# Two token halves side by side: one 512-column pass for two in q, r, the gates and the branch output projections

## The chip, the cores and the metric

One core of one Trainium2 chip runs the whole kernel. The metric is device microseconds of one launch, the median of several runs. TensorE multiplies, ScalarE (ACT) and VectorE (DVE) work element by element, GpSimd (POOL) and SyncE (SP) mostly issue transfers. Matrix products end in PSUM, whose banks hold 512 fp32 columns each.

## What is computed

One hybrid block over 256 latent tokens and 256 context tokens with 2048 channels: a modulated norm, one input projection into two mixers (GLA with 4 heads, SSD with 8 groups), a projection of each mixer's output, sigmoid gates that merge the two, an output projection, and then a product-key expert layer. Cut to what the change touches:

```
h = modulate(rmsnorm(x, w), shift, scale)
q, k, v, r, ..., z, xbc, ..., gl = split(h @ w_in)
o   = rmsnorm(o_gla) * gla_norm_w * silu(r)
y_a = o @ w_gla_out                 # 2048 -> 2048
y_b = y @ w_ssd_out                 # 4096 -> 2048
ga, gb = split(sigmoid(gl + b_gate))
out = (ga * y_a + gb * y_b) @ w_o
```

All of it is fp32. The kernel multiplies in a rounded fp32 format and keeps the precision by splitting each operand into a high part (the rounded value) and a low part (the rest). A product is then three matmuls: high x high, high x low, low x high.

## The kernel before

**Weights.** All large weights come through one `Stream` (line 27) in a fixed plan, in chunks of 128 x 1024 fp32 (512 KB): a chunk is 8 weight tiles of 128 x 128. `get` hands out a chunk and, before that, issues the load of the chunk six ahead (SyncE's queue) and the split of the chunk three ahead: ScalarE writes `hi` (line 49), VectorE writes `lo` = raw - hi (line 50). There are four `hi` and four `lo` buffers, so the split of a chunk waits until TensorE is done with the chunk four before it.

**Products.** `mm3` (lines 320 to 326) goes through the 8 tiles of a chunk and issues three matmuls for each: weight high x token high (324), weight high x token low (325), weight low x token high (326), all into the same columns of PSUM. The normalized tokens are `Hhi` and `Hlo`, 16 tiles of 512 columns each: latent tokens in columns 0 to 255 (`XT`), context tokens behind them. k, xs and B use all 512 columns (`CT`); q, r, z, C and the gates use 256. v (`v_part`, lines 332 to 334) has the tokens as stationary operand and weights of 512 columns moving.

**Banks.** Four PSUM banks rotate under the tag mm. `pair` (line 949) computes two feature tiles of 256 columns into the two halves of one bank; a unit "r" takes two pairs, a unit "v" takes four banks at once.

**Order.** `units` is a list of work written out by hand: for heads 1 to 3 it is k, k, q of the head, r of the head before, v of the head; then r of the last head; then eight groups of SSD units (xs, one gl, xs, C, xs, B, xs, z, z); then the last eight gl. After each chunk `tick` calls `step`, which first moves every background generator on by one step (GLA, decay of the next head, SSD, conv, transfers back) and after that runs the functions in `later`. `q_out`, `r_out` and `gl_out`, which empty the banks of a finished unit, go through `later`; so they are issued in the tick after the first chunk of the next unit. After that `tick` issues a ride: one product on VectorE of a modulation weight that rides along (line 368). Every engine works through its instructions in the order of issue.

**After the units.** `split_in` brings the GLA and SSD outputs back from DRAM and splits them into `yh` and `yl` (lines 986 and 987). `oproj` multiplies them, 2 chunks a feature tile for GLA and 4 for SSD, and `gated` multiplies the bank with the sigmoid of the gates (line 1070) on VectorE. Then come w_o, and the expert layer with 512-column matmuls at its end (lines 1489 to 1491).

**Lines that the prediction names.** 560: a small GLA product that waits for products on VectorE (550). 962: Silu of r out of PSUM. 969: gate plus bias out of PSUM. 494 to 503: decay on VectorE. 583: a sum in GLA. 1254: a reduction in the expert layer. 760: an operation on PSUM in SSD. 1127: sums of squares before the second norm.

Of the kernel before, what the change touches and what calls it, by code (L numbers as in the profile page):

```python
# [10 lines left out]
F32 = mybir.dt.float32  # L11
F32R = mybir.dt.float32r
U32 = mybir.dt.uint32
AF = mybir.ActivationFunctionType
OP = mybir.AluOpType
AX = mybir.AxisListType
# [3 lines left out]
P = 128  # L20
D = 2048
T = 256
KT = D // P
# [71 lines left out]
def hybrid_block_kernel(ctx, tc, A, out):  # L95
    nc = tc.nc
    ctx.enter_context(tc.manual_schedule())
    mm_ = nc.tensor.matmul
# [5 lines left out]
    st = Stream(nc, streams, 6, 3)  # L104

    def mmbank(shape=(P, 512)):
        return psum.tile(list(shape), F32, name="mm", tag="mm", bufs=4)
# [4 lines left out]
    def cload(name, shape):  # L112
        t = consts.tile(list(shape), F32, name=name)
        nc.gpsimd.dma_start(t, A[name])
        return t
# [86 lines left out]

    es_h = ExitStack()
    hpool = es_h.enter_context(tc.tile_pool(name="hh", bufs=1))
    Hhi = hpool.tile([P, KT, 512], F32R, name="Hhi")
    Hlo = hpool.tile([P, KT, 512], F32R, name="Hlo")
    es_w = ExitStack()
    w4 = es_w.enter_context(tc.tile_pool(name="w4", bufs=1, reuse_waits="tile"))
    es_x = ExitStack()
# [36 lines left out]
    b_gate = cload("b_gate", [P, 32])  # L246
# [72 lines left out]
    def mm3(ps, W2, h0, n, hi, lo, tok, start, stop):  # L319

        Whi, Wlo = (w.rearrange("p (k f) -> p k f", f=P) for w in W2)
        for j in range(n):
            k = h0 + j
            mm_(ps, Whi[:, j, :], hi[:, k, tok], start=start and j == 0, stop=False)  # L324
            mm_(ps, Whi[:, j, :], lo[:, k, tok], start=False, stop=False)  # L325
            mm_(ps, Wlo[:, j, :], hi[:, k, tok], start=False, stop=stop and j == n - 1)  # L326

    def v_part(pv, W2, k, j):
        Whi, Wlo = W2
        for tb in range(4):  # L330
            tok = slice(P * tb, P * tb + P)
            mm_(pv[tb], Hhi[:, k, tok], Whi[:, j, :], start=k == 0, stop=False)  # L332
            mm_(pv[tb], Hhi[:, k, tok], Wlo[:, j, :], start=False, stop=False)  # L333
            mm_(pv[tb], Hlo[:, k, tok], Whi[:, j, :], start=False, stop=k == KT - 1)  # L334

    def v_weights():
        return [w.rearrange("p (k f) -> p k f", k=2) for w in st.get()]
# [14 lines left out]
    def tick(riding=True):  # L352
        nonlocal ticks
        step()
        ticks += 1
        st.board()
        if riding and st.aboard and ride_n < 240:
            ride_piece()
# [30 lines left out]
    XT, CT = slice(0, 256), slice(0, 512)  # L389
# [5 lines left out]
    for k, a, b in START:  # L395
# [16 lines left out]
        elif k == "ld":  # L412
# [5 lines left out]
            for w, pp in enumerate((plr, pdt)):  # L418
                Whi, Wlo = (t[:, w, kt % 4] for t in ld)
# [26 lines left out]
    o_d = dram.tile([P, KT, T], F32, name="o_d")  # L446
    y_d = dram.tile([P, 32, T], F32, name="y_d")
# [6 lines left out]
    S = 1.0 / 16.0  # L454
# [4 lines left out]
    Qt, Vt, Rt, Bt, Xt, Ct, Zt, Bm = {}, {}, {}, {}, {}, {}, {}, {}  # L459
# [468 lines left out]
    def pair():  # L928
        ps = mmbank((P, 2, 256))
        for e in range(2):  # L930
            ftile(ps[:, e], XT)
        return ps

    def wait(what):
        while what not in ended:
            step()
# [16 lines left out]

    def q_out(a, ps):
        Qt[a] = wt("s2", [P, 2, 256])
        nc.scalar.activation(Qt[a], ps, AF.Copy, scale=S)

    def r_out(a, pr):
        Rt[a] = []
        for ps in pr:  # L960
            t = wt("s2", [P, 2, 256])
            nc.scalar.activation(t, ps, AF.Silu)
            Rt[a].append(t)
        nc.scalar.preload_act_table_set(NLE)

    def gl_out(a, ps):
        t = op.tile([P, 2, 256], F32, name="mt", tag="mt", bufs=2) if op else wt("s2", [P, 2, 256])
        for e in range(2):
            nc.scalar.activation(t[:, e], ps[:, e], AF.Identity, bias=b_gate[:, 2 * a + e:2 * a + e + 1])
        nc.gpsimd.dma_start(g_d[:, 2 * a:2 * a + 2], t)  # L970


    es_o = ExitStack()
    op = None
    ohi, olo, yhi, ylo, G = [], [], [], [], []

    def split_in(pool, src, n, hi, lo):
        for i in range(n // 4):
            t = op.tile([P, 4, T], F32, name="yr", tag="yr", bufs=2)
            nc.gpsimd.dma_start(t, src[:, 4 * i:4 * i + 4])  # L980
            if i % 2 == 0:
                hi.append(pool.tile([P, 8, T], F32R, name="yh", tag="yh", bufs=n // 8))
                lo.append(pool.tile([P, 8, T], F32R, name="yl", tag="yl", bufs=n // 8))
            s = slice(4 * (i % 2), 4 * (i % 2) + 4)
            yield
            nc.scalar.activation(hi[-1][:, s], t, AF.Copy)
            nc.vector.tensor_sub(lo[-1][:, s], t, hi[-1][:, s].bitcast(F32))

    def open_out():
        nonlocal op  # L990
# [10 lines left out]
    def to_out():  # L1001
        while ("y", 7) not in ended:
            yield
        open_out()
        yield from split_in(op, o_d, 16, ohi, olo)

    for u in units:
        kind, a, b = u
        if kind == "k":
            if b == 0 and a > 1:  # L1010
                Kt[a] = wt("s4", [P, 2, 512])
            ps = mmbank()
            ftile(ps, CT, int(a < 2))
            later.append(lambda a=a, b=b, ps=ps: k_out(a, b, ps))
        elif kind == "q":
            ps = pair()
            later.append(lambda a=a, ps=ps: q_out(a, ps))
        elif kind == "v":
            pv = [mmbank() for _ in range(4)]
            for i in range(8):  # L1020
                w2 = v_weights()
                for j in range(2):
                    v_part(pv, w2, 2 * i + j, j)
                tick()
            wait(("gla", a - 1))
            v_evac(a, pv)
        elif kind == "r":
            pr = [pair(), pair()]
            later.append(lambda a=a, pr=pr: r_out(a, pr))
        elif kind in ("xs", "B", "C"):  # L1030
            nx = 1 if kind == "C" else 2
            ps = mmbank()
            ftile(ps[:, :256 * nx], CT if nx == 2 else XT)
            f = 4 * a + b if kind == "xs" else 32 + a if kind == "B" else 40 + a
            o = wt("s1" if nx == 1 else "s2", [P, 256 * nx])
            bg.append(conv(ps, f, nx, o))
            if kind == "xs":
                Xt.setdefault(a, []).append(o)
            elif kind == "B":
                Bm[a] = o  # L1040
            else:
                Ct[a] = o
        elif kind == "z":
            Zt.setdefault(a, []).append(pair())
            if b == 1:
                if a:
                    wait(("ssd", a - 1))
                later.append(lambda a=a: silu_group(a))
                if a == 7:
                    bg.append(to_out())  # L1050
        elif kind == "gl":
            ps = pair()
            later.append(lambda a=a, ps=ps: gl_out(a, ps))
    drain()
    es_h.close()
# [7 lines left out]
    yp = es_y.enter_context(tc.tile_pool(name="yp", bufs=1, reuse_waits="tile"))  # L1063

    def gated(n, t, ps):

        gate_load(n + 2)
        if n < 15:
            nc.scalar.activation(G[1], G[1], AF.Sigmoid)
        nc.vector.tensor_mul(t, ps, G.pop(0))  # L1070

    def oproj(ps, hi, lo):
        n = len(hi)
        for h in range(n):
            mm3(ps, st.get(), 0, 8, hi[h], lo[h], slice(0, 256), h == 0, h == n - 1)

    ysplit = split_in(yp, y_d, 32, yhi, ylo)
    nc.scalar.activation(G[0], G[0], AF.Sigmoid)
    for i in range(8):
        ps = mmbank((P, 2, 256))  # L1080
        for e in range(2):
            oproj(ps[:, e], ohi, olo)
            next(ysplit, None)
        t = mp.tile([P, 2, T], F32, name="ma", tag="mx", bufs=8)
        gated(i, t, ps)
        Ma.append(t)
        step()
    for i in range(8):
        ps = mmbank((P, 2, 256))
        for e in range(2):  # L1090
            oproj(ps[:, e], yhi, ylo)
        t = op.tile([P, 2, 256], F32, name="mt", tag="mt", bufs=2)
        s = slice(2 * i, 2 * i + 2)
        gated(8 + i, t, ps)
        nc.vector.tensor_add(t, t, Ma.pop(0))
        h = mp.tile([P, 2, T], F32R, name="Mhi", tag="mx", bufs=8)
        nc.scalar.activation(h, t, AF.Copy)
        nc.vector.tensor_sub(Mlo[:, s], t, h.bitcast(F32))
        Mhi.append(h)
# [29 lines left out]
    for i in range(8):  # L1129
        ps = mmbank((P, 2, 256))  # L1130
# [6 lines left out]
        for e in range(2):  # L1137
            k = 2 * i + e
            nc.vector.scalar_tensor_tensor(x1[:, k], ps[:, e], mods[:, 0, 32 + k:33 + k], x1[:, k], op0=OP.mult, op1=OP.add)
        s = slice(2 * i, 2 * i + 2)  # L1140
# [19 lines left out]
    for k in range(KT + 2):  # L1160
# [4 lines left out]
        if k > 1:  # L1165
            j = k - 2
# [172 lines left out]
    for j, e, h in QORD:  # L1339
        if j < 2:  # L1340
            pq.setdefault((j, e), mmbank((P, 256)) if h == 0 else None)
        elif e == 0 and h == 0:
            t = mmbank((P, 2, 256))
# [119 lines left out]
    for b in range(NB):  # L1463
# [4 lines left out]
        for group in ([0], [1], [2], [3]) if b < NB - 1 else ([0], [1], [2, 3]):  # L1468
# [6 lines left out]
            ps, W2 = {}, {}  # L1475
            for order in ([(t, i, j) for i in group for j in range(2) for t in range(2)] if len(group) == 1 else
                          [(t, i, j) for t in range(2) for i in group for j in range(2)]):
                t, i, j = order
# [7 lines left out]
                for k in range(2):  # L1486
                    Whi, Wlo = (w[:, k] for w in W2[i, j])
# [87 lines left out]
```

## Time and profile before

| | us |
|---|---|
| median of 3 runs | 3643.9 |
| lowest, highest | 3643.74, 3644.59 |
| profiled execution | 3642.91 |
| its span, first to last instruction | 3641.1 |
| TensorE busy in it | 3546.8 |
| VectorE busy | 2369.1 |
| ScalarE busy | 1667.7 |

Times in rows are microseconds from the start of the span, durations in ns where marked so. An engine's busy time counts any instant with an instruction in flight; matmuls overlap, so a row of 0.28 us can be followed by the next start 0.12 us later. A bracket behind a row is the idle time of the engine before it and what ended it.

### The profile page before, as it was taken

How to read it: one execution, taken by the hardware profiler on the slowest of the kernel's cores; microseconds unless marked ns; L12 is line 12 of the kernel's file. 1: busy time of each engine (PE TensorE's matmuls, PEld its weight loads, DVE VectorE, ACT ScalarE, POOL GpSimd, SP SyncE). 2: the span in 40 equal slices, each digit the busy share in tenths (PEclk: the TensorE clock that was granted, in tenths of full speed). 3: DMA queues.
4: the chain of work that ended last, by engine and by line, in shares of the span. 5: the costliest groups of instructions: out<-in, count | busy, mean ns of one | idle time of the engine just before them, and what ended most of it. 6: DMA issues, size and time to landing. Idle time of an engine off the chain costs nothing.

```text
span 3641.1 us, 58912 instructions
## 1 busy us (share of the span) xinstructions
PE 3546.8 (97%) x23679; PEld 3182.4 (87%) x23679; DVE 2369.1 (65%) x3569; ACT 1667.7 (46%) x2226; POOL 369.9 (10%) x424
## 2 busy tenths in 40 slices
PE   5989999999999999999999999999999999999998
PEld 2578999888888888999998999999999999998886
DVE  3375665677777776656544788875555555556777
ACT  2244454355555555555433446464444444444444
POOL 0000000000000000010002016361000000000004
PEclk9999999999999999999999999999999999999999
DMA  7744555656655554467667557677666666666774
GB/s 270 263 142 158 179 166 180 194 165 206 207 195 180 180 190 150 156 222 254 194 207 234 162 178 202 196 205 223 197 197 197 198 198 198 198 197 205 235 234 146
DMA packets 214145, 715.39 MB, mean 196 GB/s; under 512 B 24688, under 2 KB 24832, under 8 KB 213360
## 3 DMA queue, kind: packets, MB, share of 16 engines
q1 hardware_dynamic: 188928, 625.04, 53.3%
q0 software_dynamic: 24944, 86.59, 8.7%
q8 instruction: 186, 3.05, 0.3%
q14 instruction: 87, 0.71, 0.1%
HBM read 679.93 MB, written 31.60 MB: 195 GB/s over the span
## 4 chain that ended last, share of the span: by engine, by line
PE 90%; DVE 5%; DMA 3%; ACT 1%; issue 1%; SPq 0%; POOL 0%; DVEq 0%; ACTq 0%; POOLq 0%
PE mm L324 19%; PE mm L326 19%; PE mm L325 19%; PE mm L1490 6%; PE mm L1489 6%; PE mm L1491 6%; PE mm L332 2%; PE sc L1296 2%; PE mm L334 2%; PE mm L333 2%; DVE lo L50 1%; PE sc L866 1%; PE sc L607 1%; PE sc L799 1%; DMA x_d<-x 1%
## 5 line engine op out<-in xcount | busy, mean ns | idle before, releaser
L50 DVE TENSOR_TENSOR lo<-raw,hi 128x1024 fp32r<-128x1024 f32 x996 | 1234.9, 1246 | 1044.4 <-ACT hi L49 1040.7
L49 ACT ACTIVATE hi<-raw 128x1024 fp32r<-128x1024 f32 x996 | 1046.8, 1058 | 1410.8 <-PE mm L325 640.1
L324 PE MATMUL mm<-Hhi,hi 128*128 128x256 f32 (+1 forms) x2272 | 735.3, 324 | 2.2 <-ACT hi L49 1.4
L326 PE MATMUL mm<-Hhi,lo 128*128 128x256 f32 (+1 forms) x2272 | 722.0, 318 | 0.9 <-DVE lo L50 0.9
L325 PE MATMUL mm<-Hlo,hi 128*128 128x256 f32 (+1 forms) x2272 | 721.9, 318 | 0.0
L324 PE MATMUL mm<-h2hi,hi 128*128 128x256 f32 x2304 | 656.3, 285 | 0.0
L325 PE MATMUL mm<-h2lo,hi 128*128 128x256 f32 x2304 | 651.9, 283 | 1.6 <-DVE h2lo L1167 1.1
L326 PE MATMUL mm<-h2hi,lo 128*128 128x256 f32 x2304 | 651.1, 283 | 0.0
L324 PEld LDWEIGHTS mm<-Hhi,hi 128*128 128x128 f32 x2272 | 433.3, 191 | 38.2 <-issue 5.5
L325 PEld LDWEIGHTS mm<-Hlo,hi 128*128 128x128 f32 x2272 | 433.4, 191 | 30.4 <-issue 1.9
L326 PEld LDWEIGHTS mm<-Hhi,lo 128*128 128x128 f32 x2272 | 433.0, 191 | 30.6 <-DVE lo L50 1.2
L325 PEld LDWEIGHTS mm<-h2lo,hi 128*128 128x128 f32 x2304 | 441.2, 191 | 5.8 <-DVE h2lo L1167 2.6
L324 PEld LDWEIGHTS mm<-h2hi,hi 128*128 128x128 f32 x2304 | 440.9, 191 | 4.1 <-ACT h2hi L1164 0.8
L326 PEld LDWEIGHTS mm<-h2hi,lo 128*128 128x128 f32 x2304 | 440.9, 191 | 0.0
L1490 PE MATMUL mm<-lo,ph 128*128 128x512 f32 x1024 | 405.9, 396 | 4.5 <-DVE lo L50 4.5
L1489 PE MATMUL mm<-hi,ph 128*128 128x512 f32 x1024 | 406.1, 397 | 0.0
L1491 PE MATMUL mm<-hi,pl 128*128 128x512 f32 x1024 | 404.8, 395 | 0.0
L1490 PEld LDWEIGHTS mm<-lo,ph 128*128 128x128 f32 x1024 | 192.7, 188 | 48.6 <-DVE lo L50 6.0
L1491 PEld LDWEIGHTS mm<-hi,pl 128*128 128x128 f32 x1024 | 192.8, 188 | 46.5
L1489 PEld LDWEIGHTS mm<-hi,ph 128*128 128x128 f32 x1024 | 193.0, 188 | 43.0
L326 PE MATMUL mm<-yh,lo 128*128 128x256 f32 x768 | 217.0, 283 | 1.5 <-DVE lo L50 1.5
L324 PE MATMUL mm<-yh,hi 128*128 128x256 f32 x768 | 216.9, 282 | 0.7 <-ACT hi L49 0.7
(337 smaller groups left out, 4558.4 us busy)
## 6 DMA issues: line engine op xcount, KB each, us to landing
raw<-in_w_f_dram SPq DMA_DIRECT2D x288, 512.0 KB, 3.7
raw<-in_u_dram SPq DMA_DIRECT2D x256, 512.0 KB, 4.1
raw<-in_v_dram SPq DMA_DIRECT2D x256, 512.0 KB, 4.1
ride<-in_w_ada_dram SPq DMA_DIRECT2D x240, 256.0 KB, 4.0
raw<-in_w_so_dram SPq DMA_DIRECT2D x64, 512.0 KB, 4.1
raw<-in_w_ada_dram SPq DMA_DIRECT2D x45, 512.0 KB, 6.8
raw<-in_w_v_dram SPq DMA_DIRECT2D x32, 512.0 KB, 3.6
s<-cum_d POOLq DMA_DIRECT2D x64, 256.0 KB, 6.3
```

Source lines behind the costliest of these rows:

```text
L49: self.nc.scalar.activation(hi, t, AF.Copy)
L50: self.nc.vector.tensor_sub(lo, t, hi.bitcast(F32))
L324: mm_(ps, Whi[:, j, :], hi[:, k, tok], start=start and j == 0, stop=False)
L325: mm_(ps, Whi[:, j, :], lo[:, k, tok], start=False, stop=False)
L326: mm_(ps, Wlo[:, j, :], hi[:, k, tok], start=False, stop=stop and j == n - 1)
L332: mm_(pv[tb], Hhi[:, k, tok], Whi[:, j, :], start=k == 0, stop=False)
L333: mm_(pv[tb], Hhi[:, k, tok], Wlo[:, j, :], start=False, stop=False)
L334: mm_(pv[tb], Hlo[:, k, tok], Whi[:, j, :], start=False, stop=k == KT - 1)
L1296: mm_(pg[:, j], o1[:, j], o2[:, j], start=True, stop=True)
L1489: mm_(ps[t, i], ghi, Whi, start=j == 0 and k == 0, stop=False)
L1490: mm_(ps[t, i], ghi, Wlo, start=False, stop=False)
L1491: mm_(ps[t, i], glo, Whi, start=False, stop=j == 1 and k == 1)
```

## The change

For q, r, the gates and both branch output projections the high and the low token part lie side by side in one tile, and one matmul of 512 columns takes the high weight part over both: columns 0 to 255 of the bank collect products with the high part, columns 256 to 511 those with the low part. The low weight part still takes 256 columns, into the lower half. The order of the last two is turned so that the 512-column matmul is last. A feature tile so fills a whole bank, and a pair two banks. The halves are added on VectorE by a reduction (`both`) out of PSUM into SBUF, before ScalarE's copy, Silu or bias, or before the product with the gate. `Hhi` and `Hlo` become views of one tile `H`, in which high and low of a row tile lie 512 columns apart. `z`, `C`, the 512-column units, v, w_o and the expert layer stay.

```diff
-    Hhi = hpool.tile([P, KT, 512], F32R, name="Hhi")
-    Hlo = hpool.tile([P, KT, 512], F32R, name="Hlo")
+    H = hpool.tile([P, KT, 2, 512], F32R, name="H")
+    Hhi, Hlo = H[:, :, 0], H[:, :, 1]
...
+    def mm2(ps, W2, h0, x, start, stop):
+        Whi, Wlo = (w.rearrange("p (k f) -> p k f", f=P) for w in W2)
+        for j in range(8):
+            k = h0 + j
+            last = stop and j == 7
+            for w in (Wlo, Whi) if last else (Whi, Wlo):
+                if w is Whi:
+                    mm_(ps, w[:, j, :], x[:, k], start=start and j == 0, stop=last)
+                else:
+                    mm_(ps[:, 0:256], w[:, j, :], x[:, k, 0], start=False, stop=False)
+
+    def both(out, ps):
+        nc.vector.tensor_reduce(out, ps.rearrange("p (s t) -> p t s", s=2), axis=AX.X, op=OP.add)
...
+    def wide_pair():
+        pss = []
+        for e in range(2):
+            pss.append(mmbank())
+            for h in range(2):
+                mm2(pss[e], st.get(), 8 * h, H[:, :, :, XT], h == 0, h == 1)
+                tick()
+        return pss
...
     def q_out(a, ps):
         Qt[a] = wt("s2", [P, 2, 256])
-        nc.scalar.activation(Qt[a], ps, AF.Copy, scale=S)
+        for e in range(2):
+            both(Qt[a][:, e], ps[e])
+        nc.scalar.activation(Qt[a], Qt[a], AF.Copy, scale=S)
...
-        for ps in pr:
+        for h in range(2):
             t = wt("s2", [P, 2, 256])
-            nc.scalar.activation(t, ps, AF.Silu)
+            for e in range(2):
+                both(t[:, e], pr[h][e])
+            nc.scalar.activation(t, t, AF.Silu)
...
         for e in range(2):
-            nc.scalar.activation(t[:, e], ps[:, e], AF.Identity, bias=b_gate[:, 2 * a + e:2 * a + e + 1])
+            both(t[:, e], ps[e])
+            nc.scalar.activation(t[:, e], t[:, e], AF.Identity, bias=b_gate[:, 2 * a + e:2 * a + e + 1])
...
-                hi.append(pool.tile([P, 8, T], F32R, name="yh", tag="yh", bufs=n // 8))
-                lo.append(pool.tile([P, 8, T], F32R, name="yl", tag="yl", bufs=n // 8))
+                to.append(pool.tile([P, 8, 2, T], F32R, name="y2", tag="y2", bufs=n // 8))
...
         elif kind == "q":
-            ps = pair()
+            ps = wide_pair()
...
-            pr = [pair(), pair()]
+            pr = [wide_pair(), wide_pair()]
...
         elif kind == "gl":
-            ps = pair()
+            ps = wide_pair()
...
-        nc.vector.tensor_mul(t, ps, G.pop(0))
+        for e in range(2):
+            both(t[:, e], ps[e])
+        nc.vector.tensor_mul(t, t, G.pop(0))
...
+    def oproj(x):
+        ps = mmbank()
+        for h in range(len(x)):
+            mm2(ps, st.get(), 0, x[h], h == 0, h == len(x) - 1)
+        return ps
```

## Rows read from the trace of the kernel before

**Rows 1.** The page: busy time by engine, and the chain that ended last.
```profile
PE 3546.8 (97%) x23679; PEld 3182.4 (87%) x23679; DVE 2369.1 (65%) x3569; ACT 1667.7 (46%) x2226; POOL 369.9 (10%) x424
...
PE 90%; DVE 5%; DMA 3%; ACT 1%; issue 1%; SPq 0%; POOL 0%; DVEq 0%; ACTq 0%; POOLq 0%
```

**Rows 2.** Busy time in stretches (PE, PEld, DVE, ACT, POOL); timeline of TensorE.
```profile
1720.00:1800.00 80.00, 80.00 (x669) 80.00 (x669) 40.27 (x37) 31.94 (x35) 1.61 (x3) 1.00 0.64 194
3400.00:3480.00 80.00, 80.00 (x344) 64.43 (x343) 57.54 (x64) 32.83 (x32) 6.27 (x12) 1.00 0.75 247
...
348.84 0.39 PE L324 MATMUL mm<-Hhi,hi 128*128 128x512 f32 x1
...
351.79 0.39 PE L325 MATMUL mm<-Hlo,hi 128*128 128x512 f32 x1
```

**Rows 3.** Timeline of TensorE from k (512 columns) to q (256).
```profile
370.37 0.39 PE L326 MATMUL mm<-Hhi,lo 128*128 128x512 f32 x1
370.60 0.28 PE L324 MATMUL mm<-Hhi,hi 128*128 128x256 f32 x1
```

**Rows 4.** Instructions by line and shape: count, busy us, mean ns, idle before.
```profile
L324 PE MATMUL mm<-Hhi,hi 128*128 128x256 f32 x1536 | 443.3, 289 | 1.4 <-ACT hi L49 1.4
```

**Rows 5.** Timeline of TensorE and VectorE in q and r of the first heads.
```profile
260.92 0.75 DVE L368 SCALAR_TENSOR_TENSOR ride<-ride,cS 128x512 f32<-128x512 f32 x1 [2.52 <-DMA ride<-in_w_ada_dram]
...
265.37 1.13 PE L560 MATMUL sc<-s,s 128*128 128x128 f32 x8 [2.12 <-DVE s L550]
...
274.43 1.40 PE L560 MATMUL sc<-s,s 128*128 128x128 f32 x7 [2.19 <-DVE s L550]
```

**Rows 6.** Groups by line: a reduction, and an operation on PSUM.
```profile
L1254 DVE TENSOR_REDUCE tok<-eq 128x64 f32<-128x1024 f32 x8 | 9.7, 1207 | 0.0
L760 DVE TENSOR_TENSOR s<-sc,tm 128x512 f32<-128x512 f32 x64 | 41.1, 683 | 13.1 <-PE sc L754 13.1
```

**Rows 7.** Timeline from r of head 0 to v of head 1.
```profile
293.85 0.40 PE L332 MATMUL mm<-hi,Hhi 128*128 128x512 f32 x1
...
296.96 0.50 PE L332 MATMUL mm<-hi,Hhi 128*128 128x512 f32 x1 [1.55 <-ACT s L962]
...
295.03 1.23 DVE L50 TENSOR_TENSOR lo<-raw,hi 128x1024 fp32r<-128x1024 f32 x1 [0.16 <-ACT hi L49]
```

**Rows 8.** Timeline from r of head 1 to v of head 2.
```profile
421.62 0.58 PE L332 MATMUL mm<-hi,Hhi 128*128 128x512 f32 x1
...
426.40 0.67 DVE L502 TENSOR_TENSOR_SCAN s<-ones,s 128x255 f32<-128x255 f32 x1
```

**Rows 9.** Timeline from r of head 2 to v of head 3.
```profile
539.19 0.58 PE L332 MATMUL mm<-hi,Hhi 128*128 128x512 f32 x1
...
543.15 0.66 DVE L502 TENSOR_TENSOR_SCAN s<-ones,s 128x255 f32<-128x255 f32 x1
```

**Rows 10.** Timeline from r of head 3 to the first xs.
```profile
609.62 0.40 PE L324 MATMUL mm<-Hhi,hi 128*128 128x512 f32 x1
...
612.75 0.42 DVE L583 TENSOR_TENSOR s<-Df,Db 128x256 f32<-128x256 f32 x1
```

**Rows 11.** Stretches (the figure after POOL is the granted clock); waits of TensorE.
```profile
265.00:272.00 7.00, 6.63 (x56) 6.67 (x56) 4.97 (x12) 5.94 (x15) 0.00 (x0) 1.00 0.54 185
275.00:278.00 3.00, 3.00 (x16) 3.00 (x16) 3.00 (x5) 1.06 (x1) 0.00 (x0) 0.50 0.22 69
2001.00:2006.00 5.00, 5.00 (x28) 1.74 (x32) 1.85 (x4) 3.68 (x5) 1.54 (x3) 0.66 0.35 140
...
PE sc L1127 <- ACT x1q L1145: 3.7, 1, 3.7
```

**Rows 12.** Timeline from the last gates to the projections.
```profile
1618.76 1.23 DVE L987 TENSOR_TENSOR yl<-yr,yh 128x1024 fp32r<-128x1024 f32 x1 [2.58 <-ACT yh L986]
...
1619.35 1.05 ACT L49 ACTIVATE hi<-raw 128x1024 fp32r<-128x1024 f32 x1
...
1620.45 0.39 PE L324 MATMUL mm<-yh,hi 128*128 128x256 f32 x1 [0.71 <-ACT hi L49]
```

More of the change, by code (lines that the diff above doesn't have):

```diff
@@ L974, in hybrid_block_kernel, with split_in @@
     op = None
-    ohi, olo, yhi, ylo, G = [], [], [], [], []
-    def split_in(pool, src, n, hi, lo):
+    o2, y2, G = [], [], []
+    def split_in(pool, src, n, to):
         for i in range(n // 4):
@@ L981, in split_in @@
             if i % 2 == 0:
-                hi.append(pool.tile([P, 8, T], F32R, name="yh", tag="yh", bufs=n // 8))
-                lo.append(pool.tile([P, 8, T], F32R, name="yl", tag="yl", bufs=n // 8))
+                to.append(pool.tile([P, 8, 2, T], F32R, name="y2", tag="y2", bufs=n // 8))
             s = slice(4 * (i % 2), 4 * (i % 2) + 4)
             yield
-            nc.scalar.activation(hi[-1][:, s], t, AF.Copy)
-            nc.vector.tensor_sub(lo[-1][:, s], t, hi[-1][:, s].bitcast(F32))
+            nc.scalar.activation(to[-1][:, s, 0], t, AF.Copy)
+            nc.vector.tensor_sub(to[-1][:, s, 1], t, to[-1][:, s, 0].bitcast(F32))
     def open_out():
@@ L1004, in to_out @@
         open_out()
-        yield from split_in(op, o_d, 16, ohi, olo)
+        yield from split_in(op, o_d, 16, o2)
     for u in units:
@@ L1069, in gated @@
             nc.scalar.activation(G[1], G[1], AF.Sigmoid)
-        nc.vector.tensor_mul(t, ps, G.pop(0))
[L1072 to L1077, printed above, removed]
+        for e in range(2):
[6 more added lines that the diff above has]
+        return ps
+    ysplit = split_in(yp, y_d, 32, y2)
     nc.scalar.activation(G[0], G[0], AF.Sigmoid)
     for i in range(8):
-        ps = mmbank((P, 2, 256))
+        ps = []
         for e in range(2):
-            oproj(ps[:, e], ohi, olo)
+            ps.append(oproj(o2))
             next(ysplit, None)
@@ L1088, in hybrid_block_kernel @@
     for i in range(8):
-        ps = mmbank((P, 2, 256))
-        for e in range(2):
-            oproj(ps[:, e], yhi, ylo)
+        ps = [oproj(y2) for e in range(2)]
         t = op.tile([P, 2, 256], F32, name="mt", tag="mt", bufs=2)
```

## The prediction

> **What bounds the kernel now.** I read the page first: TensorE is busy 97% of the span and is 90% of the chain that ended last [rows 1]. Busy time is no rate here, because matmuls overlap, so next come start-to-start times. In the branch output projections 669 matmuls of 256 columns start in 80 us, 119.6 ns apart. On the same tile H, 14 matmuls of 512 columns start between 348.84 and 351.79 us, 13 steps of 226.9 ns. In the last stage 512-column matmuls start 232.6 ns apart (344 in 80 us) [rows 2]. So 256 more columns cost 107.3 ns, which is 0.419 ns a column, and 119.6 - 107.3 = 12.3 ns is a fixed part of every matmul. Where a 512-column run turns into a 256-column run, the first 256-column matmul starts 0.23 us after the last 512-column one [rows 3]: the turn costs nothing extra. TensorE is therefore bound by columns, and a pass saved is worth 12.3 ns, not the 289 ns that the grouped lines call the mean of one matmul [rows 4]. Then I read the waits where PSUM banks change hands, on all three engines.
>
> **The matmuls.** Per weight tile of 128 rows, 3 x 256 columns become 512 + 256: the same 768 columns, one matmul less. The touched tiles: q 4 x 2 x 16 = 128, r 4 x 4 x 16 = 256, gates 16 x 2 x 16 = 512, together 896 of the 1536 on H; the other 640 are z and C and stay. The output projections have 16 x (2 + 4) x 8 = 768. Sum 1664 tiles, 1664 x 12.3 ns = 20.5 us. Not all of it comes through. In q and r of the first heads TensorE twice stands 2.1 to 2.2 us waiting for VectorE (line 560), which is itself paced by transfers [rows 5]; what the 10 chunks before the second wait save (10 x 8 x 12.3 ns = 1.0 us) only lengthens that wait. In the last two chunks of r of heads 1 and 2 VectorE sets the pace (below): 4 x 0.1 us. Left: 19.1 us. No row shows a moving operand in two runs of 256 columns, as H now gives; I take the pace of the one-run 512 on the same tile, 226.9 ns, and keep the last stage's 232.6 as the bad end: (3 x 119.6 - 119.6 - 232.6) = 6.6 ns, 11.0 us in all, 9.6 after the losses.
>
> The Trainium skill, page "TensorE: Matmul & The Clock Gate", section "Back-to-back issue gap", speaks against even this gain: it gives an isolated gap of N/2.4 + 2.5 ns, by which a saved pass is worth 2.5 ns, as an estimate from that page 4.2 us in all. The rows disagree: by it 256 columns would take 109.2 ns and they take 119.6.
>
> **The reduction on VectorE.** Each pair of feature tiles now needs two `both`, 88 in all (q 8, r 16, gates 32, projections 32). No row shows a reduction out of PSUM with a stride. The nearest are the reduction of 1024 elements in SBUF, 1207 ns, half of which is 0.60 us, and an operation on 512 PSUM elements, 683 ns [rows 6]; I take 0.65 us, with 0.6 and 1.2 as ends. 88 x 0.65 = 57 us more on an engine that is 65% busy [rows 1], hidden behind TensorE wherever the bank is not wanted at once. ScalarE's operations stay, out of SBUF; its gate operation and the product in `gated` keep their place in the order.
>
> **The banks.** This is where it costs. A pair held one of the four banks and now holds two; r holds two pairs, so all four. In the gate and projection stages two or more chunks (2.9 us each, 24 x 119.6 ns) lie between a pair's end and the reuse of its banks; in q, r wants q's banks four chunks later. I cost those at nothing; if VectorE were late there, each would cost its lateness. But after r comes v, which opens all four banks at its first chunk, and after the last r comes xs, which takes r's first bank. Before, r's two banks were v's third and fourth, and xs got a free one. `r_out` is emitted only in the tick after that first chunk, behind the background work of that step. So on VectorE the first `both` stands behind the split `lo` of the chunk fetched by v (itself behind `hi` on ScalarE, which waits for r's end), and behind what the step issues; TensorE cannot start v until it is done. The four places, with 0.65 us for the first `both`:
> - r0 to v1: `lo` starts at 295.03 and takes 1.23, nothing else in that step, so the bank is free near 296.95. TensorE could start v at 293.85: a wait of 3.1 us, where it now waits 1.55 us for Silu at the third bank [rows 7]. Net +1.5.
> - r1 to v2: VectorE works off decay of the next head; after `lo` come a subtraction and scans, the last of them at 426.40 for 0.67, so the first `both` ends near 427.7. TensorE now starts v at 421.62 [rows 8]. +6.1.
> - r2 to v3: the same, the last scan at 543.15 for 0.66, `both` to 544.4; v now starts at 539.19 [rows 9]. +5.2.
> - r3 to xs: after `lo`, GLA's copies and their sum to 613.17, `both` to 613.8; xs now starts at 609.62 [rows 10]. +4.2.
> Sum 17.0 us. The later banks follow at 0.65 us each against 3 x 0.227 = 0.68 us of matmuls per bank, so they don't add. With 0.6 us per `both` the sum stays 17; with 1.2 it is 17.0 + 4 x 0.55 + 3 x 3 x 0.52 = 24. If VectorE's queue ran 0.75 us ahead of these times at each place, it would be 14. Queued behind the waiting `both` on VectorE are only the ride product and later splits, three chunks ahead of use; behind ScalarE's waiting Silu is a split that v's long chunks (5.4 us) cover.
>
> **The clock.** After the 2.2 us wait at line 560 the granted clock is 0.50 in a stretch where it had been 1.00, that is 1.2 for 2.4 GHz; over the 5 us from 2001, after a wait of 3.7 us, the mean is 0.66, so 3.4 us at half [rows 5, 11]. Such a stretch costs 1.7 us. The other wait at line 560, 2.1 us, is followed by full clock. Of the new waits three are over 4 us (3 x 1.7) and one is 3.1, counted half: 6.0 us. Ends: 0 and 8.
>
> **Gates to projections.** `gl_out` on ScalarE now waits for VectorE. At the last gates this matters: VectorE runs the split `yl` from 1618.76 to 1619.99, after which two `both` end near 1621.3 and ScalarE's second gate op near 1621.7; queued behind it is the `hi` that now starts at 1619.35 and for whose end TensorE waits at 1620.45 [rows 12]. That is 2.35 us later. What slack behind it takes back, and what the last `gl_out` with its table load adds in the same way, I take to cancel: 2.3, with 0 and 5 as ends.
>
> **Sum**, against the profiled execution (3642.9 us, span 3641.1): -19.1 + 17.0 + 6.0 + 2.3 = +6.2. On the median of the runs, 3643.9, which is 1.0 above, that is 3650.1; I forecast 3650. About 0.2% (7.3 us: 3636.6 to 3651.2) is what a measurement of this kernel can tell from no change, so this is just within it.
>
> **Rivals.** (1) *The banks don't bind*: VectorE gets to `r_out` before TensorE needs the banks. Then -19.1 + 2.3 = -16.8, 3627. For it: VectorE is idle a third of the time, and r's first bank is complete six chunks earlier. Against it: the order of emission, and VectorE's queue at r1 and r2, with no idle bracket on its last scans. It decides if the first `both` ends before r does. 0.15. (2) *Slower by the wide pass*: the 512-column passes run at the last stage's 232.6 ns, as two runs of H or as y2. The gain falls to 9.6 and the sum is +15.7: 3660. For it: the same operation has that pace in the last stage. Against it: the one-run passes over H show 226.9. From 228 ns a wide pass on, with the waits as summed, the result is over 0.2% slower. 0.21. (3) *The fixed part is not saved*: if a fifth of the 12.3 ns goes with a pass and the rest stays, the gain is near 4 and the sum +21: 3665. Against it: 226.9 is not 2 x 119.6. This is what the Trainium skill's 2.5 ns ("TensorE: Matmul & The Clock Gate", "Back-to-back issue gap") would make of it. 0.04.
>
> **How the numbers follow.** My case has 0.60 and its own range 3640 to 3658 (waits 14 to 24, clock 0 to 8, tail 0 to 5, not all at one end): 0.38 of it within 0.2%, 0.20 slower, 0.02 faster. Rival 1 gives 0.15 faster, rival 2 0.19 slower and 0.02 same, rival 3 0.04 slower. Sum: faster 0.17, same 0.40, slower 0.43. The range for 8 in 10 is 3632 to 3662: it leaves out most of rival 1 and rival 3.
>
> **What would show it.** In the profile after: starts in the projections 227 and 120 ns apart, and that stage (96 chunks) 9 us shorter; TensorE waiting on the new reduction at v's first line three times and once at xs, 3 to 6 us each, followed by clock rows at half; reductions near 0.65 us; ScalarE's gate op waiting on VectorE near 1620 us. I am wrong on the gain if wide starts are 232 or more apart, on the cost if TensorE's waits on the reduction sum to less than 10 us, and on the clock if no half-clock stretch follows them.

## The result, and the profile after

The changed kernel takes 3670.1 us (median of 4 runs, 3665.8 to 3673.0), the kernel before 3644.2 us beside it (4 runs): ratio 1.0071, 95% interval 1.0059 to 1.0083. It is slower by about 26 us, 0.7%. I had forecast 3650 with 3632 to 3662, so the time lies 8 us above the range. The profiled execution took 3671.2 us, its span is 3669.4 us: 28.3 more than the span before.

A wide pass is here a 512-column matmul of `mm2`, a narrow one a matmul of 256 columns. Five landmarks of the trace cut the span: the first matmul of the first k (line 324; 198.8 us before, 195.7 after), ScalarE's first and last conv operation (after the linear attention, after the last group's conv), the first matmul of the output projections and the first of w_o. The stages in us, of the kernels before and after and of the runs told below; each is read from one profiled execution:

| kernel | median us | ratio to before | attention | eight groups | to projections | projections |
|---|---|---|---|---|---|---|
| before | 3644.2 | | 426.3 | 862.6 | 132.9 | 277.3 |
| after | 3670.1 | 1.0071 | 450.2 | 860.1 | 145.6 | 274.6 |
| e1_narrow_gates | 3661.4 | 1.0051 | 450.5 | 862.5 | 134.0 | 273.9 |
| e2_narrow_qr | 3646.0 | 1.0006 | 424.0 | 860.1 | 141.9 | 274.8 |
| e3_early_sums | 3646.0 | 1.0010 | 425.0 | 860.0 | 143.3 | 274.6 |
| e4_gate_bias_vector | 3666.7 | 1.0066 | 448.9 | 859.9 | 141.3 | 274.2 |
| e5_blocks | 3667.6 | 1.0064 | 447.2 | 859.9 | 145.4 | 271.4 |
| e6_one_tick | 3665.9 | 1.0065 | 444.7 | 859.9 | 137.1 | 277.4 |
| e7_early_groups | 3633.2 | 0.9975 | 423.8 | 859.9 | 133.6 | 274.2 |
| e8_early_groups_blocks | 3628.7 | 0.9965 | 423.1 | 859.9 | 135.2 | 269.5 |

The kernel before took 3644.2 us beside the change, 3643.7 beside e1 to e4 and 3642.1 beside e5 to e8, so across these the ratios compare and not the medians. One launch of e6 took 7253 us where its other four took 3664.7 to 3667.1, and is left out of its median and ratio.

After against before: +23.9 in the attention stage, -2.5 in the groups, +12.7 from the last conv to the projections, -2.7 in the projections, together +31.4. The start was 3.1 shorter; in the nine kernels with the change it lies between 194.3 and 197.1, in the one execution of the kernel before at 198.8, and I count it to no term. From w_o on it is 1743.4 before and 1743.3 after. How far a stage moves by itself can be seen too: the attention stage is the same code in the kernel after, e1, e4 and e6, and took 444.7 to 450.5.

The page first, as [rows 1]. The columns are busy us, share of the span and count:

```profile
PE 3548.4 (97%) x22015; PEld 3101.8 (85%) x22015; DVE 2422.6 (66%) x3657; ACT 1671.4 (46%) x2226; POOL 371.4 (10%) x424
```

There are 1664 matmuls fewer, as the diff says, and yet TensorE is busy 1.6 us longer: its busy share again says nothing. The reductions, grouped by line and tile (count, busy us, mean ns; these are 52 of the 88):

```profile
L343 DVE TENSOR_REDUCE s<-mm 128x256 f32<-128x512 f32 x52 | 33.0, 683 | 0.0
```

Now TensorE's waits over the whole span (us in total, times, longest). Those on L343 and L917 are new; waits for `hi` and `lo` were there before, but shorter (in the last two stages 2.1 us for `hi`, 2.4 for `lo`).

```profile
PE mm L349 <- DVE s L343: 14.2, 3, 6.0
PE sc L923 <- POOL s L917: 5.9, 1, 5.9
PE mm L337 <- ACT hi L49: 5.4, 2, 5.2
PE mm L324 <- DVE s L343: 4.2, 1, 4.2
PE mm L337 <- DVE s L343: 2.1, 1, 2.1
PE mm L339 <- DVE lo L50: 3.7, 6, 1.1
```

L349 is v's first line, L324 here xs, L337 a wide pass, L339 a narrow one, L923 the sum over the last group's Y for its norm, L343 `both`. The timeline of TensorE gives the places, answering [rows 7 to 10] in their order; the second line is VectorE's at r1:

```profile
295.90 0.50 PE L349 MATMUL mm<-hi,H 128*128 128x512 f32 x1 [3.01 <-DVE s L343]
...
428.32 0.69 DVE L343 TENSOR_REDUCE s<-mm 128x256 f32<-128x512 f32 x1
...
429.06 0.80 PE L349 MATMUL mm<-hi,H 128*128 128x512 f32 x1 [6.03 <-DVE s L343]
...
553.29 0.74 PE L349 MATMUL mm<-hi,H 128*128 128x512 f32 x1 [5.20 <-DVE s L343]
...
629.00 0.77 PE L324 MATMUL mm<-H,hi 128*128 128x512 f32 x1 [4.24 <-DVE s L343]
```

One more such wait stands at 243.53 us (2.06): the second q wants the banks of the first, whose sums come late behind other work of VectorE.

After each of the four the granted clock falls to 0.5, that is 1.2 GHz, for a while. Windows right behind the four; the figure after POOL's is the granted clock:

```profile
296.00:300.50 4.50, 4.50 (x14) 3.59 (x15) 2.31 (x4) 2.54 (x3) 0.00 (x0) 0.65 0.50 179
429.20:436.00 6.80, 6.80 (x21) 5.42 (x22) 2.26 (x4) 2.54 (x3) 0.00 (x0) 0.65 0.12 45
553.40:557.00 3.60, 3.60 (x9) 2.83 (x10) 2.29 (x4) 2.54 (x3) 0.00 (x0) 0.53 0.28 108
628.20:632.00 3.80, 3.00 (x7) 2.44 (x8) 3.10 (x6) 1.93 (x3) 0.00 (x0) 0.55 0.89 326
```

What a window lost is its length times (1 - clock): 1.6 + 2.4 + 1.7 + 1.7 = 7.4 us.

The stretch from the last group to the projections, on all engines. First what leads to the norm, then what leads to the first projection:

```profile
1601.53 2.47 DVE L50 TENSOR_TENSOR lo<-raw,hi 128x1024 fp32r<-128x1024 f32 x2
1604.77 1.28 DVE L343 TENSOR_REDUCE s<-mm 128x256 f32<-128x512 f32 x2
1605.48 1.11 ACT L1000 ACTIVATE s<-s,b_gate 128x256 f32<-128x256 f32 x2 [2.75 <-DVE s L343]
1606.50 1.04 ACT L49 ACTIVATE hi<-raw 128x1024 fp32r<-128x1024 f32 x1
1607.58 1.23 DVE L50 TENSOR_TENSOR lo<-raw,hi 128x1024 fp32r<-128x1024 f32 x1 [1.53 <-ACT hi L49]
1608.72 0.48 DVE L889 SCALAR_TENSOR_TENSOR s<-s,dskip,sc 128x256 f32<-128x256 f32 x1
1609.69 1.06 ACT L915 ACTIVATE s<-s 128x1024 f32<-128x1024 f32 x1 [2.15 <-DVE s L890]
1612.17 1.59 POOL L917 TENSOR_TENSOR s<-s 128x256 f32<-128x256 f32 x1
1613.81 1.22 PE L923 MATMUL sc<-s,ones 128*128 128x256 f32 x2 [5.87 <-POOL s L917]
...
1627.96 0.57 POOL L1001 DMA_DIRECT2D g_d<-s  x1 [3.77 <-ACT hi L49]
1634.10 0.54 POOL L1029 DMA_DIRECT2D gt<-g_d  x1 [5.04 <-DMA g_d<-s]
1634.64 1.06 POOL L1011 DMA_DIRECT2D yr<-o_d  x2
1639.42 1.06 ACT L1016 ACTIVATE y<-yr 128x1024 fp32r<-128x1024 f32 x1 [12.45 <-issue]
1641.48 0.80 PE L337 MATMUL mm<-H,hi 128*128 128x512 f32 x1 [5.24 <-ACT hi L49]
```

And the same matmul with its suppliers in the kernel before, where it starts without a bracket, 1.2 us after GpSimd is done; the first row stands at the gate pair before:

```profile
1575.14 2.36 DVE L50 TENSOR_TENSOR lo<-raw,hi 128x1024 fp32r<-128x1024 f32 x2 [3.13 <-ACT hi L49]
...
1584.98 0.47 DVE L872 SCALAR_TENSOR_TENSOR s<-s,dskip,sc 128x256 f32<-128x256 f32 x1
...
1588.46 0.74 POOL L900 TENSOR_TENSOR s<-s 128x256 f32<-128x256 f32 x1
...
1590.38 0.59 PE L906 MATMUL sc<-s,ones 128*128 128x256 f32 x2
```

The reader is to see a round trip that was not there. The last Y evacuation (L889) of the last group stands behind two sums, which ScalarE's gate operation waits for, behind which `hi` is queued, for which VectorE's `lo` waits: 1.28 + 1.53 = 2.81 us for this gate pair. In the kernel before that evacuation (L872) starts 5.4 us ahead of L906; here it starts 0.8 us behind the time when TensorE was ready for L923 (1613.81 - 5.87 = 1607.94). It is 6.2 us late, and GpSimd's last sum takes 1.59 instead of 0.74. Less the 1.2 of slack, that is the wait of 5.87. Of the 6.2 the last round trip is 2.81. The rest was there ahead of it, and the earlier gate pairs' shares are not separated: they are not 2.81 each, since at the pair before VectorE stood 3.13 us for `hi` in the kernel before too.

Then comes the clock, and a second wait. The gate store L1001 is late, and the second reload of gates (L1029) waits for it to land. The loads of `yr`, the GLA output, stand behind it on GpSimd. ScalarE's split of `yr` (L1016) waits for them, and behind it stands the `hi` of a chunk of the last gates, for which TensorE waits 5.24 us. Windows behind the two waits:

```profile
1614.00:1618.00 4.00, 4.00 (x12) 3.33 (x13) 0.84 (x1) 0.89 (x2) 0.00 (x0) 0.50 0.81 217
...
1641.00:1652.00 11.00, 9.70 (x33) 7.48 (x33) 7.09 (x8) 5.91 (x8) 1.61 (x3) 0.63 0.55 196
```

They cost 4 x 0.5 + 11 x 0.37 = 6.1 us.

Last the pace in the projections, as [rows 2]:

```profile
1700.00:1780.00 80.00, 80.00 (x457) 69.73 (x457) 51.08 (x53) 36.44 (x39) 4.29 (x8) 1.00 0.70 231
1800.00:1880.00 80.00, 80.00 (x455) 69.49 (x454) 44.89 (x44) 33.45 (x36) 1.61 (x3) 1.00 0.62 199
```

From start to start a wide pass there takes 235.1 ns and a narrow one 117.8 (means of 732 and 736 steps), 352.9 for a weight tile that took 3 x 119.6 = 358.8.

### The profile page after: what moved, and what is told of

Its sections match the earlier page's. It is cut to its first block, busy times and chain, and to the rows that moved or that the text cites. A ratio compares the mean times of both kernels' runs of the same rounds, so it can differ in the third digit from the quotient of the medians.

```text
span 3669.4 us, 55691 instructions
## 1 busy us (share of the span) xinstructions
PE 3548.4 (97%) x22015; PEld 3101.8 (85%) x22015; DVE 2422.6 (66%) x3657; ACT 1671.4 (46%) x2226; POOL 371.4 (10%) x424
## 4 chain that ended last, share of the span: by engine, by line
PE 50%; DVE 2%; DMA 2%; issue 1%; ACT 1%; DVEq 0%; POOL 0%; ACTq 0%; POOLq 0%
PE mm L325 8%; PE mm L326 8%; PE mm L324 8%; PE mm L1520 6%; PE mm L1521 6%; PE mm L1522 6%; PE mm L337 5%; PE mm L339 2%; PE sc L1327 2%; DVE lo L50 1%; DMA raw<-in_w_o_dram 1%; DMA x_d<-x 1%; ACT hi L49 0%; DMA raw<-in_v_dram 0%; PE sc L1252 0%
## 5 line engine op out<-in xcount | busy, mean ns | idle before, releaser
L324 PE MATMUL mm<-h2hi,hi 128*128 128x256 f32 x2304 | 656.3, 285 | 0.0
L324 PE MATMUL mm<-H,hi 128*128 128x512 f32 (+1 forms) x1376 | 476.9, 347 | 5.1 <-DVE s L343 4.2
L326 PE MATMUL mm<-H,lo 128*128 128x512 f32 (+1 forms) x1376 | 468.2, 340 | 0.0
L325 PE MATMUL mm<-H,hi 128*128 128x512 f32 (+1 forms) x1376 | 468.2, 340 | 0.0
L324 PEld LDWEIGHTS mm<-h2hi,hi 128*128 128x128 f32 x2304 | 440.9, 191 | 4.1 <-issue 0.8
L337 PE MATMUL mm<-H,hi 128*128 128x512 f32 x896 | 329.3, 408 | 7.3 <-ACT hi L49 5.2
L324 PEld LDWEIGHTS mm<-H,hi 128*128 128x128 f32 x1376 | 261.2, 190 | 40.1 <-issue 9.3
L325 PEld LDWEIGHTS mm<-H,hi 128*128 128x128 f32 x1376 | 261.4, 190 | 29.7 <-issue 1.7
L326 PEld LDWEIGHTS mm<-H,lo 128*128 128x128 f32 x1376 | 261.1, 190 | 29.4
L337 PE MATMUL mm<-y,hi 128*128 128x512 f32 x768 | 268.7, 397 | 0.2 <-ACT hi L49 0.2
L339 PE MATMUL mm<-H,lo 128*128 128x256 f32 x896 | 245.0, 284 | 0.9 <-DVE lo L50 0.9
```

The lines of the kernel that those rows point to most:

```text
L337: mm_(ps, w[:, j, :], x[:, k], start=start and j == 0, stop=last)
L339: mm_(ps[:, 0:256], w[:, j, :], x[:, k, 0], start=False, stop=False)
```

## The experiments

**Narrow gates.** All 16 gate pairs go back to the narrow form.

```diff
-            both(t[:, e], ps[e])
-            nc.scalar.activation(t[:, e], t[:, e], AF.Identity,
+            nc.scalar.activation(t[:, e], ps[:, e], AF.Identity,
...
-            ps = wide_pair()
+            ps = pair()
```

> One part undone: the 16 gates go back to a pair in one bank, evacuated by ScalarE alone; q, r and the projections stay wide. Theory A (in the last gates ScalarE stands behind VectorE's new sums, and everything that hangs on ScalarE is late): the stretch from the last conv to the first projection matmul, 12.7 us longer after the change, goes back, and the eight groups lose their 2.5 us of gain, so about 3660. Rival B (the loss there comes from the way back of the SSD output into the new tile of high and low parts, which stays): 3670 within 4.

Measured: 3661.4 us, ratio 1.0051 (1.0034 to 1.0067). The stretch to the projections is back at 134.0, GpSimd's sum is in time and at full pace and the matmul has no bracket:

```profile
1608.16 0.74 POOL L917 TENSOR_TENSOR s<-s 128x256 f32<-128x256 f32 x1
...
1610.16 0.59 PE L923 MATMUL sc<-s,ones 128*128 128x256 f32 x2
```

So the wide gates are what the stretch lost by, and not the way back of the SSD output, which is rival B. Whether it is by ScalarE's wait, as theory A says, this run does not tell. The gates had gained 2.5 us in the groups, which is gone too.

**Narrow q and r.** The same for these two; gates and projections stay wide.

> One part undone: q and r go back to pairs in one bank; gates and projections stay wide. Theory A (v and the first xs wait for r's sums, 16 to 18 us, and each wait is followed by a stretch at half clock): the 24 us by which the first xs came later go, about 3646. Rival B (the extra time there is the clock of the start and the new layout of H, which stays): above 3660.

Measured: 3646.0 us, ratio 1.0006 (0.9997 to 1.0016). The attention stage is at 424.0, beside 426.3 before. The wide q and r cost 26 us there, 24 by the medians, and more than 90% of the change's loss went with them; the gates' tail and the gains elsewhere nearly cancel. In that tail, whose gates are those of the kernel after, TensorE stands 5.80 us at L923 again, but the reload does not wait for the gate store, and TensorE waits for `hi` 1.9 us later on and 2.9 at the first projection, instead of 5.2 and 0.2.

**Early sums of r.** r stays wide, but each bank is summed as soon as its tile ends, the last one ahead of the split of v's first chunk.

```diff
+            if t is not None and now and e == 1:
+                both(t[:, e], pss[e])
+            elif t is not None:
+                later.append(lambda e=e, ps=pss[e]: both(t[:, e], ps))
...
-            for e in range(2):
-                both(t[:, e], pr[h][e])
```

> All of the change stays, but r's sums are issued one by one, each in the tick after its feature tile, and the last one right behind r's last tick, ahead of the next chunk's split. Theory A (it is the place of the sums in VectorE's queue that holds the banks): TensorE's waits on the sum at v and xs fall from 20 us to under 3, and the half-clock stretches behind them go: about 3648. Rival B (VectorE is simply too full there): the delay goes over to the splits, TensorE waits on lo instead, time above 3662.

Measured: 3646.0 us, ratio 1.0010 (1.0000 to 1.0020), 2 us below the 3648 that theory A gave. The waits on the sum, and the window from r of head 0 to the last r:

```profile
PE mm L349 <- DVE s L343: 2.1, 2, 1.4
PE mm L337 <- DVE s L343: 2.1, 1, 2.1
...
290.00:620.00 330.00, 327.94 (x1671) 279.92 (x1670) 204.68 (x323) 150.66 (x235) 4.33 (x8) 1.00 0.49 167
```

14.2 + 4.2 became 2.1 with the same matmuls and the same 16 reductions of r, and the half-clock stretches behind the four waits are gone: the granted clock is 1.00 throughout. So it is the place of the sums in VectorE's queue, not the two banks more nor the sums themselves, that costs.

**Gate bias on VectorE.** ScalarE then waits for no sum, but the bias operation moves to VectorE.

```diff
-            nc.scalar.activation(t[:, e], t[:, e], AF.Identity, bias=...)
+            nc.vector.tensor_scalar(t[:, e], t[:, e], b_gate[...], None, op0=OP.add)
```

> All of the change stays, but the gate's bias is added on VectorE right behind the sum, so that ScalarE has no gate operation and waits for no sum there. Theory A (ScalarE behind VectorE makes the last gates late): TensorE's wait of 5.9 us on GpSimd's sum of squares falls under 1.5 and the time falls by 8 to 13, about 3659. Rival B (VectorE itself is late there): 0.35 us more per feature tile on VectorE make it no better, 3668 or more.

Measured: 3666.7 us, ratio 1.0066 (1.0049 to 1.0082), between the two. The wait at L923 is 4.6 instead of 5.9; I had expected less than 1.5. VectorE's rows, and the wait:

```profile
1603.80 0.68 DVE L343 TENSOR_REDUCE s<-mm 128x256 f32<-128x512 f32 x1
1604.52 0.35 DVE L1000 TENSOR_SCALAR s<-s,b_gate 128x256 f32<-128x256 f32 x1
1604.79 0.68 DVE L343 TENSOR_REDUCE s<-mm 128x256 f32<-128x512 f32 x1
1605.51 0.35 DVE L1000 TENSOR_SCALAR s<-s,b_gate 128x256 f32<-128x256 f32 x1
1605.77 1.22 DVE L50 TENSOR_TENSOR lo<-raw,hi 128x1024 fp32r<-128x1024 f32 x1
...
1612.00 1.22 PE L923 MATMUL sc<-s,ones 128*128 128x256 f32 x2 [4.58 <-POOL s L917]
```

The 1.53 us of standing for `hi` is gone, but sums and biases hold VectorE 1605.77 - 1603.80 = 1.97 us where sums and standing held it 2.81. That is 0.84 us for each of the last two pairs ahead of L923, 1.7; the wait fell by 1.3. ScalarE's part of the round trip is 1.53 us and the sums' own time 1.28, so that taking the one out and putting two biases in gains little. My theory A, that ScalarE's wait alone is the cause, fell.

**One tick more ahead of the norm.**

```diff
         yield
+        yield
         if g < 7:
             yield
-            yield
         pm = scbank((P, 256))
```

> After the change, with one more tick (one weight chunk, 2.8 us) between the squares of the last group's Y and the matmul with ones that sums them (three ticks in every other group, one in the last, here two). Theory A (the 12.7 us that the stretch from the last group's last gates to the projections lost hang on this one matmul: TensorE stands 5.9 us for the sum on GpSimd and then runs at half clock, and all that follows is late by that): the wait falls below 3.1 us, the half-clock stretch near 1614 us is gone, the stretch from the last conv to the first projection falls from 145.6 to 138 to 140 us, whole 3663 to 3665. Theory B (the queues of VectorE and ScalarE are late by the sums, and a later y only moves the wait to the first projection's split): the wait at the matmul goes but the one before the first projection grows from 5.2 us by as much, whole 3668 to 3671.

Measured: 3665.9 us, ratio 1.0065 (1.0049 to 1.0080). One row of TensorE:

```profile
1608.68 1.22 PE L923 MATMUL sc<-s,ones 128*128 128x256 f32 x2 [2.98 <-POOL s L917]
```

A tick of 2.8 us took 2.9 off the wait, half of it. The stretch fell by 8.5 us to 137.1: the gate store now goes out ahead, the reload no longer waits for it, and TensorE's later wait for `hi` is 0.7 us. But half clock remains behind the 3 us wait, and the projections became 2.8 us longer, with a wait of 1.8 us on `y` and 3.4 us at half clock from 1645.4. By the ratios this run can't be told from the kernel after, since the intervals overlap. Theory A holds for the wait and the stretch, not for the half clock; for the whole, its 3663 to 3665 lies 1 us below the median, which settles nothing.

**Passes in blocks.** In `mm2` seven wide passes, then the eight narrow ones, then the last wide one.

```diff
-        for j in range(8):
-            ...
+        for j in range(7):
+            mm_(ps, Whi[:, j, :], x[:, h0 + j], start=start and j == 0, stop=False)
+        for j in range(8):
+            mm_(ps[:, 0:256], Wlo[:, j, :], x[:, h0 + j, 0], start=False, stop=False)
+        mm_(ps, Whi[:, 7, :], x[:, h0 + 7], start=False, stop=stop)
```

> After the change, with one thing altered: within a weight chunk mm2 issues seven wide passes in a row, then the eight narrow ones, then the last wide one, where the kernel after alternates wide and narrow. Theory A (the alternation is what makes the wide pass of this kernel start-to-start 231 to 236 ns, where runs of 512 columns on H have 227): wide starts inside a run near 227 ns, narrow ones 119.6, some 4 ns per weight tile on 1664 tiles, and the four waits of 0.5 to 1.3 us on lo in the projections shrink because lo is wanted later in the chunk: projections 268 to 271 us (after: 274.6), whole 3660 to 3665. Theory B (the pace belongs to the pass itself, from its two runs of columns or its fp32 pair): wide starts stay at 231 to 236, projections 271 to 275 us by the lo waits alone, whole 3666 to 3671.

Measured: 3667.6 us, ratio 1.0064 (1.0050 to 1.0078); projections 271.4. A stretch of them, to be set beside the count of 455 in the kernel after:

```profile
1790.00:1870.00 80.00, 80.00 (x461) 70.49 (x460) 46.06 (x45) 33.45 (x36) 1.61 (x3) 1.00 0.62 202
```

From start to start at full clock a wide pass inside a run now takes 231.3 ns (mean of 664 steps), a narrow one 119.3, and the last wide one before the narrow ones 228.6. That is between the theories: out of the alternation a wide pass is 4 ns shorter and a narrow one 1.5 longer, 2.3 ns less a tile, and the 227 of [rows 2] is not reached. The waits on `lo` in the projections fell from 2.8 to 0.2 us, because `lo` is wanted later in its chunk, but 2.2 us on `hi` came in their place. For the whole the gain can't be told from none, as the intervals overlap; the next pair shows it better.

**Both repairs.** e7: early sums of r, and wide gates only in the groups, the last eight pairs narrow. e8: e7 with the passes in blocks.

> After the change, with two parts altered: r's halves are summed as each of its tiles ends, ahead of the next split (as in the run e3_early_sums), and the last eight gate pairs, those behind the last group, are narrow again with ScalarE reading the bank (as all gates were in e1_narrow_gates); q, r, the first eight gates and the projections stay wide. Theory A (the losses are two separate ones, r's sums behind v's split and the tail, and they add up): e3 measured 3646.0 and the tail gives back 9.5 to 11 us, so 3635 to 3637, below the kernel before (3643.7) by 0.2%; waits of TensorE on L343 near 4 us in all, none at the matmul of the norm, stretch from last conv to first projection 133 to 135 us. Theory B (they share a cause, such as VectorE's load over the whole kernel): 3641 to 3646.

> The run e7_early_groups with the order of e5_blocks as well. If alternating widths costs the 4 ns per weight tile: 5 to 7 us below e7_early_groups, near 3630. If the pace belongs to the wide pass itself: within 3 us of e7_early_groups.

Measured: e7 3633.2 us, ratio 0.9975 (0.9964 to 0.9986); e8 3628.7 us, ratio 0.9965 (0.9953 to 0.9977). Both are faster than the kernel before, by 0.25 and 0.35%, with intervals that leave out 1. The two losses add up as theory A of e7 said: it came out 2 us below its range, beside a kernel before that was 1.6 us below the 3643.7 it reckoned with. In e7 TensorE's waits on `both` are 4.1 us in all, and none stands at L923. e8 is 4.5 us below e7, a little less than its first theory's 5 to 7, and the projections show where: 269.5 against 274.2, 4.7 us. Of these 2.1 are waits on `lo` (2.3 against 0.2 us), and 768 x 2.9 ns = 2.2 the pace (231.3 + 119.3 = 350.6 ns for a tile, against 235.4 + 118.1 = 353.5). So alternating costs 3 ns a tile, not the 4 that I gave it, and the rest is where `lo` is wanted. Some of it is lost again ahead of the projections, where e8 has 6.8 us at half clock from 1604.4 us and e7 3.4 from 1607.3. In e8's list of waits these remain of the change (L340 is `both` there, L346 v's first line, L333 a wide pass, L335 a narrow one):

```profile
PE mm L346 <- DVE s L340: 2.1, 2, 1.5
PE mm L333 <- DVE s L340: 2.0, 1, 2.0
PE mm L335 <- DVE lo L50: 0.2, 1, 0.2
```

## Why the prediction was wrong, step by step

**A pass is worth 12.3 ns: mis-sized.** It saved 5.9 ns per tile in the projections, and 2.5 us / 256 tiles = 9.8 ns in the groups. With 9.8 for all tiles on H that is, as an estimate, 768 x 5.9 + 896 x 9.8 ns = 13.3 us, where I had 20.5 before and 19.1 after the losses. What failed is the choice of the price: I took 226.9 ns from one run of equal 512-column passes, and "the turn costs nothing extra" from one turn [rows 3]. This kernel turns at every pass. My own bad end, the last stage's 232.6 ns and 6.6 a tile, was nearer, and the projections are below even that; rival 2 had this part right by its number. Two runs of columns in the moving operand can't be the reason there: the projections' tile has one run, where H has two. Blocks took back part; what sets the rest stays open.

**The reduction: right.** 0.68 us where I had 0.65.

**The banks: right.** 3.01, 6.03, 5.20 and 4.24 us against 3.1, 6.1, 5.2 and 4.2; with the old Silu wait gone 16.9 where I had 17.0. e3 shows the reason to be the one given: the place behind the split in VectorE's queue. Missed beside it: 2.06 us where the second q wants the first one's banks. I had put q's and r's reuse at nothing, by counting chunks and not by reading where VectorE stood at that time.

**The clock: right in kind, too small.** 7.4 us at the four places for 6.0. Another 1.0 stands around 238 to 250 us (0.52 where it had been 0.60 over 12 us), but e1, with the same code there, has the half clock of the kernel before, 10.2 us, so that this is not shown to be the change's. The 3.01 us wait, counted half, was followed by half clock in full, and the 6.03 one by a longer stretch (2.4 us lost) than the 1.7 I took from [rows 11].

**Gates to projections: this step failed.** I had 2.3 us, with 5 as the worst end, and a gain of 256 passes beside it. The stretch lost 12.7. TensorE's waits in it, the one at its end included, went from 3.05 to 12.15 us, the clock took 6.1, and the passes gave back about 2.5: together 12.7. I had asked of the gate pairs only whether their banks are free in time, and for the last of them whether the projections' first split is late [rows 12]. I did not ask what else stands behind their sums on VectorE: the Y evacuation, whose chain by ScalarE and GpSimd to L923 had 1.2 us to spare in the last group, where it gets one tick and not three. The rows for it were in the trace of before. e1 and e7 show that the last gates are the cause, e4 and the round trip of 2.81 us that both engines' queues have a part in it, e6 that a tick of 2.8 us pays for half of the wait at L923.

**The projections: mis-sized by the same 12.3.** 768 x 12.3 = 9.4 us were to come, 2.7 came: 4.5 by the pace, less 1.3 for `lo`, whose waits grew from 1.5 to 2.8 us, and 0.5 that I can't place. I had costed the sums at nothing there, hidden behind TensorE, and by the banks they are, as no wait on L343 stands in this stage. The waits for `lo` I had not asked about; e5 shows that they go when `lo` is wanted later in the chunk.

By terms: -13.3 for the passes, +16.9 at the banks, +2.1 at q, -0.6 at the two old waits [rows 5] (4.3 to 3.7 us), +8.4 clock there, +9.1 and +6.1 in the tail, +1.3 for `lo`: +30.0, against the +31.4 of the stages. Against my +6.2 the tail is 13 us of the miss, the passes 6, the clock 2, q and `lo` 3. Of the three signs that I named, one came out against me (wide starts at 232 or more), and none watched the norm of the last group.

## What to carry to other kernels

When an operation is added to an engine with time to spare, go through everything that is queued behind it and through the next engine's queue too, and find the chain with the least slack; whether the buffers come free in time is only one of the questions, and the last turn of a loop, where there are fewer ticks, is where it binds first. A sum that frees a bank belongs ahead of work that waits for something later: issuing r's sums tile by tile, the last of them ahead of one split, was worth about 24 us with nothing else changed. And a rate read from equal instructions in a row is not the rate of a mixture.

## What the runs showed of the hardware that I had not expected

A 512-column matmul starts its successor after 227 ns in the runs of 512 on H, 231 in blocks of seven and 235.1 where 512 and 256 columns alternate in the projections, all at full granted clock; the 256-column one in the alternation takes 117.8 where it takes 119.6 among its own kind.

GpSimd's sum of 256 elements took 0.74 us in the kernel before, e1, e7 and e8, and 1.59 in the kernel after, where it starts in the midst of two splits on VectorE that together took 3.12 us instead of 2.36:

```profile
1611.72 3.12 DVE L50 TENSOR_TENSOR lo<-raw,hi 128x1024 fp32r<-128x1024 f32 x2 [2.07 <-ACT hi L49]
```

In the kernel before GpSimd started first and the split beside it took 1.55 instead of 1.22. The Trainium skill, page "SBUF — State Buffer", section "SBUF: two separate sides", describes the port pair of VectorE and GpSimd as an exclusive lock: of a VectorE operation with two SBUF inputs and a GpSimd operation that reads SBUF, the one that starts first has it for its whole length, and the other stands. These rows agree with that, with 0.85 us lost by GpSimd's sum and 0.76 by the two splits; no run here tested it alone.
